# Strassen's scheme for both feed-forwards of a hybrid streaming encoder step

## The chip, the cores and the metric

One core of one Trainium2 chip runs the whole program. The metric is device time in microseconds (us) of one execution, the median of the runs. PE is the TensorE matmul engine, PEld its weight load, DVE the VectorE, ACT the ScalarE, POOL the GpSimd and SP the SyncE, whose queue issues all DMAs here.

## The reference

One encoder layer for 1024 prompt tokens and 64 sample tokens (1088 columns together), model width 1024, hidden width 2816, all in float32:

```
h = x + 1/2 * SwiGLU_1(RMSNorm(x))
h = h + concat(A, B, C) @ w_out          # gated units, pooling, gated delta rule
h = h + CrossAttn(RMSNorm(h))
h = h + 1/2 * SwiGLU_2(RMSNorm(h));  y = RMSNorm(h)
swiglu(h) = (silu(h @ w_gate) * (h @ w_up)) @ w_down
```

The two SwiGLU blocks are what changes. The norm's factor of a token is applied after the gate and up products, its gain to the operand before them.

## The kernel before, in words

Activations lie with features on partitions: a tile is 128 features by 1088 tokens. x has 8 tiles, the hidden layer 22. A float32 product is made of three products of two float32r parts, high x high, high x low and low x high (`mm3`, L219; its matmul is L224, the line of nearly all of PE's work). Tokens go in three chunks `CH` of 364, 362 and 362 columns, one PSUM bank each. A weight unit of 512 columns is loaded by SP (`load`, L195) and cut into its two parts by `weights` (L200): ACT copies the high part (`copy_act`, L159), DVE subtracts it for the low part (`tt`, L171). `product` (L210) makes 128 output columns from two units and the eight tiles of x.

`ffn` (L328) goes through the 22 hidden tiles in pairs. `gate(f)` (L332) makes a product, multiplies it by the norm's factor from PSUM (DVE, L171), applies Silu (ACT, L337) and multiplies once more (POOL, L171). `up(f, sg)` (L341) makes the other product, multiplies it in (DVE) and cuts the hidden tile (ACT, DVE). Then the pair's share of the down product is added to all eight tiles of h, which stay in SBUF (`stt`, L174, DVE from PSUM). In the last pair `done` prepares what follows: `done1` (L383) the mixers' operand, `done_att` (L1128) the second feed-forward's operand, by `split_x` (L258) and `add_square` (L264). In the second feed-forward the last pair goes chunk by chunk (`CF`), so that the final norm can begin.

Between the feed-forwards lie the mixers (L459) and the cross-attention (L1038), whose last step is `project` (L1135): `residual` adds its products to h by tiles of m, half 0 and half 1 (steps W0 and W1 of `ORDER2`).

The program's order on each engine is set by a planner that takes instructions by program order and by when it thinks them ready; each engine then runs its own list strictly in order. The first loads and cuts are written out by hand (`LOADS`, `CUTS`). Buffers are rings: an allocation waits for the last reader of the place.

Of the kernel before, what the change touches and what calls it, by code (L numbers as in the profile page):

```python
# [15 lines left out]
P = 128  # L16
TP = 1024          # prompt tokens
TS = 64            # sample tokens
# [10 lines left out]
WR = 3  # L29
WS = 4  # L30
CV = 8
NC = 2
# [26 lines left out]
RS = 3  # L59
EX = 1  # L60
XT = 2
HB = 9
LOADS = "v0 x00 g0 x01 u0 x02 x1 x2 x3 g1 u1 x4 x5 x6 x7 c0"
CUTS = "x00 g0 x01 u0 x02 x1 s0 x2 s1 x3 s2 g1 x4 u1 s3 x5 s4 x6 s5 x7 s6 s7"
A0 = (2, 4, 6, 7)
A1 = (6,7)
# [29 lines left out]
class Pool:  # L96
    """Tiles of 9 * 2^k columns: sizes that nest, so that the packing of SBUF leaves no gaps."""
# [4 lines left out]
    def tile(self, shape, dt, **kw):  # L102
        cols, c = 1, 9
        for n in shape[1:]:
            cols *= n
        while c < cols:
            c *= 2
        t = self.pool.tile([shape[0], c], dt, **kw)[:, :cols]
        return t.rearrange("p (a b) -> p a b", b=shape[2]) if len(shape) > 2 else t


class Slots:
    """Small tiles within a large one, each tag's in turn."""
# [4 lines left out]
    def tile(self, shape, dt, name, tag=None, bufs=1):  # L118
        cols = 1
        for n in shape[1:]:  # L120
            cols *= n
        ring = self.tags.setdefault(tag or name, [])
        if len(ring) < bufs:
            t = self.t[:, self.end:self.end + cols]
            self.end += cols
            ring.append(t.rearrange("p (a b) -> p a b", b=shape[2]) if len(shape) > 2 else t)
        else:
            ring.append(ring.pop(0))
        return ring[-1]


@with_exitstack
def encoder_step(ctx: ExitStack, tc: tile.TileContext, a):
# [16 lines left out]
    def banks(main, small, norm="sp"):  # L150
        """The eight PSUM banks, divided between the large products and the rest."""
# [18 lines left out]
    def tt(eng, out, in0, in1, op):  # L170
        eng.tensor_tensor(out=out, in0=in0, in1=in1, op=op)  # L171
# [22 lines left out]

    def load(src, w=512, tag="wr", bufs=WR):  # L195
        r = wp.tile([P, 528], F32, name=tag, tag=tag, bufs=bufs)
        sp.dma_start(r[:, :w], src)
        return r

    def weights(src, w=512, r=None):  # L200
        """A weight unit of w columns, loaded and cut exactly into two float32r parts."""
        if r is None:
            r = load(src, w)
        hi = wp.tile([P, 528], F32R, name="wh", tag="wh", bufs=WS)
        lo = wp.tile([P, 528], F32R, name="wl", tag="wl", bufs=WS)
# [4 lines left out]
    def product(units, x, chunks=CH):  # L210
        """w.T x for 128 columns of w and eight tiles of x, in PSUM banks by chunk."""
# [7 lines left out]
    def mm3(pp, w, c0, x, first, last, chunks=CH, m=P):  # L219
        """out += w.T x in float32: three products of the float32r parts, over all chunks."""  # L220
# [4 lines left out]

    def segs(s, n):
        """A chunk's columns as runs within the prompt or the sample: (in chunk, token, length)."""
# [4 lines left out]
    # ------------------------------------------------------------ constants  # L232
    fixed = const.tile([P, C_N + V_N + P + 1 + 264 + 8 * P], F32, name="fixed")
    cst, rest = fixed[:, :C_N], fixed[:, C_N:]
# [3 lines left out]
    row, rest = rest[:, :264], rest[:, 264:]  # L238
    wsg = rest[:, :4 * P].rearrange("p (h f) -> p h f", f=P)
    bsg = rest[:, 4 * P:6 * P].rearrange("p (t f) -> p t f", f=P)  # L240
    wpl = rest[:, 6 * P:].rearrange("p (t f) -> p t f", f=P)
# [16 lines left out]
    def split_x(src, g, slots, s=0, w=NT):  # L258
        hi, lo = (t[:, s:s + w] for t in slots)
        copy_act(hi, src[:, s:s + w], g)  # L260
# [3 lines left out]
    def add_square(acc, src, first, s=0, w=NT, eng=pool):  # L264
        """acc += src * src"""
        if first:
            act.activation(out=acc[:, s:s + w], in_=src[:, s:s + w], func=ACTF.Square)
            return
        sq = cvtile()[:, :w] if w > 512 else npool.tile([P, 512], F32, name="sq", tag="sq", bufs=3)[:, :w]
        act.activation(out=sq, in_=src[:, s:s + w], func=ACTF.Square)  # L270
        tt(eng, acc[:, s:s + w], acc[:, s:s + w], sq, ALU.add)

    def inv_rms(acc, rs=None, chunks=CH):
        """1/rms of every token, on all partitions."""
# [8 lines left out]
    def rms_tile():  # L283
        return npool.tile([P, NT], F32, name="rs", tag="rs", bufs=RS)
# [14 lines left out]
    def rows_tile():  # L299
        rt = npool.tile([P, 9], F32, name="rt", tag="rt", bufs=3)  # L300
# [3 lines left out]
    def all_rows(rt, rs):  # L304
        """A scalar of each token, tokens on partitions: on all partitions."""
        for c0, c1, w in ((0, 4, P), (4, 8, P), (8, 9, TS)):
            dg = npool.tile([P, 512], F32, name="sq", tag="sq", bufs=3)
# [20 lines left out]
    def ffn(h, x, rs, wg, wu, wd, done, chunks=None, first=None):  # L328
        with ExitStack() as fc:
            fp = mk("ffn", fc)  # L330

            def gate(f):  # L332
                sg = cvtile()[:, :NT]
                pp = first[0] if f == 0 and first else product([wg[f, 0], wg[f, 1]], x)
                for i, (s, n) in enumerate(CH):
                    tt(dve, sg[:, s:s + n], pp[i][:, :n], rs[:, s:s + n], ALU.mult)
                act.activation(out=sg, in_=sg, func=ACTF.Silu)  # L337
                tt(pool, sg, sg, rs, ALU.mult)
                return sg

            def up(f, sg):  # L341
                pp = first[1] if f == 0 and first else product([wu[f, 0], wu[f, 1]], x)
                for i, (s, n) in enumerate(CH):
                    tt(dve, sg[:, s:s + n], pp[i][:, :n], sg[:, s:s + n], ALU.mult)
                hi = fp.tile([P, NT], F32R, name="fh", tag="fh", bufs=4)
                lo = fp.tile([P, NT], F32R, name="fl", tag="fl", bufs=4)
                copy_act(hi, sg)
                tt(dve, lo, sg, hi.bitcast(F32), ALU.subtract)
                return hi, lo

            sg = gate(0)
            for f0 in range(0, NF, 2):
                # the next group's first product runs while this one's last operand is made
                hid = [up(f0, sg), up(f0 + 1, gate(f0 + 1))]
                if f0 < NF - 2:
                    sg = gate(f0 + 2)
                if f0 == NF - 2 and chunks:
                    # the last one chunk by chunk, so that what follows can begin
                    ws = [weights(wd[f0 // 2, mm]) for mm in range(4)]
                    for s, n in chunks:  # L360
                        for m in range(8):
                            pp = [main_ps()]
                            for j in range(2):
                                mm3(pp, ws[m // 2], j * 256 + (m % 2) * P, hid[j], j == 0, j == 1, ((s, n),))
                            stt(h[m][:, s:s + n], pp[0][:, :n], 0.5, h[m][:, s:s + n], ALU.mult, ALU.add)
                            done(m, s, n)
                    continue
                for mm in range(4):
                    w = weights(wd[f0 // 2, mm])
                    for m in (2 * mm, 2 * mm + 1):  # L370
                        pp = [main_ps() for _ in CH]
                        for j in range(2):
                            mm3(pp, w, j * 256 + (m % 2) * P, hid[j], j == 0, j == 1)
                        for i, (s, n) in enumerate(CH):
                            stt(h[m][:, s:s + n], pp[i][:, :n], 0.5, h[m][:, s:s + n], ALU.mult, ALU.add)
                        if f0 == NF - 2:
# [949 lines left out]
```

## Time and profile before

| | |
|---|---|
| median of 3 runs | 2359.32 us (2356.23 to 2359.63) |
| profiled execution, span | 2359.1 us (no other time of that execution is given) |
| instructions | 35138 |
| TensorE granted clock | 9 tenths or more of full speed in all 40 slices of the page |
| DMA | 144.31 MB, 61 GB/s on average |

Rows of groups read as: line, engine, operation, output <- inputs by the program's names (pp: main PSUM tiles, wr: raw weights, wh and wl: their parts, x: operand tiles, h: residual tiles, cv: work tiles), shapes, count, busy time and mean of one, then the idle time before them and what ended it. A release marked "<-DVE h L171" means that the engine sat idle until that instruction finished.

### The profile page before, as it was taken

What the parts mean: (1) busy time and instruction counts of PE and PEld (TensorE: products, weight loads), DVE (VectorE), ACT (ScalarE), POOL (GpSimd) and SP (SyncE); (2) the same over time, 40 slices, a digit from 0 to 9 for tenths busy, and PEclk for the clock granted to TensorE, in tenths of its full rate; (3) what the DMA queues carried; (4) which work ended last, traced back from release to release, by engine and by line L of the source; (5) the groups of instructions that cost most, each with busy time, mean ns of one, the idle gap of its engine ahead of it and who ended that gap; (6) DMA issues with size and microseconds to landing.
All of it is one profiled execution on the core that took longest, in us unless ns stands there. A gap on an engine that the chain in (4) does not pass through costs nothing.

```text
span 2359.1 us, 35138 instructions
## 1 busy us (share of the span) xinstructions
PE 2322.1 (98%) x14161; PEld 2258.7 (96%) x14161; DVE 1214.2 (51%) x2754; ACT 680.6 (29%) x1375; POOL 280.6 (12%) x231
## 2 busy tenths in 40 slices
PE   9999999999999999999999999999999999999997
PEld 8999999999999999898888999899999999999997
DVE  6443343443344657786867565864333334333346
ACT  5111111111111466545544444631111111111113
POOL 2000000000000210110230120110000000000005
PEclk9999999999999999999999999999999999999999
DMA  5111111111111212111114431311111111111102
GB/s 173 45 45 41 47 43 41 50 45 46 42 40 45 104 49 84 46 38 57 61 54 149 170 134 42 115 50 45 46 45 45 41 45 45 45 45 45 41 23 76
DMA packets 82166, 144.31 MB, mean 61 GB/s; under 512 B 14916, under 2 KB 28364, under 8 KB 82004
## 3 DMA queue, kind: packets, MB, share of 16 engines
q1 hardware_dynamic: 82004, 142.07, 18.7%
q8 instruction: 111, 1.82, 0.3%
q14 instruction: 51, 0.42, 0.1%
HBM read 119.19 MB, written 22.85 MB: 60 GB/s over the span
## 4 chain that ended last, share of the span: by engine, by line
PE 94%; DVE 4%; ACT 1%; DMA 1%; issue 0%; SPq 0%; POOL 0%; DVEq 0%; POOLq 0%; ACTq 0%
PE pp L224 83%; PE aux L490 1%; DVE x L174 1%; PE g L738 1%; PE g L733 1%; DVE wl L171 1%; DVE yo L174 1%; PE po L1106 1%; PE sc L1092 1%; PE pp L962 0%; PE g L715 0%; DVE pw L171 0%; PE sw L772 0%; PE sw L768 0%; PE sw L776 0%
## 5 line engine op out<-in xcount | busy, mean ns | idle before, releaser
L224 PE MATMUL pp<-x,wh 128*128 128x362 f32 (+2 forms) x6016 | 1220.3, 333 | 12.2 <-DVE h L171 5.2
L224 PEld LDWEIGHTS pp<-x,wh 128*128 128x128 f32 x6016 | 1025.1, 190 | 24.8 <-issue 5.5
L224 PE MATMUL pp<-x,wl 128*128 128x364 f32 (+2 forms) x3008 | 694.0, 333 | 0.0
L224 PEld LDWEIGHTS pp<-x,wl 128*128 128x128 f32 x3008 | 525.2, 190 | 4.3 <-issue 2.2
L159 ACT ACTIVATE wh<-wr 128x512 fp32r<-128x512 f32 (+2 forms) x360 | 207.4, 612 | 706.7 <-PE pp L224 513.8
L174 DVE SCALAR_TENSOR_TENSOR h<-pp,h 128x364 f32<-128x364 f32 (+3 forms) x528 | 250.6, 529 | 216.5 <-PE pp L224 216.5
L171 DVE TENSOR_TENSOR wl<-wr,wh 128x512 fp32r<-128x512 f32 (+2 forms) x360 | 276.7, 773 | 120.0 <-ACT wh L159 119.5
L171 POOL TENSOR_TENSOR cv<-cv,rs 128x1088 f32<-128x1088 f32 x44 | 111.4, 2533 | 1384.1 <-ACT cv L337 1244.2
L171 DVE TENSOR_TENSOR cv<-pp,rs 128x362 f32<-128x362 f32 (+2 forms) x225 | 100.9, 493 | 336.0 <-PE pp L224 336.0
L224 PE MATMUL pp<-fh,wh 128*128 128x362 f32 (+4 forms) x1056 | 240.1, 331 | 3.2 <-DVE h L174 3.1
L224 PE MATMUL pp<-fl,wh 128*128 128x362 f32 (+4 forms) x1056 | 240.3, 331 | 0.0
L224 PE MATMUL pp<-fh,wl 128*128 128x362 f32 (+4 forms) x1056 | 239.8, 331 | 0.0
L171 DVE TENSOR_TENSOR cv<-pp,cv 128x364 f32<-128x364 f32 x129 | 61.1, 529 | 270.7 <-PE pp L224 270.7
L224 PEld LDWEIGHTS pp<-fh,wh 128*128 128x128 f32 x1056 | 184.7, 189 | 4.4 <-DVE h L174 3.9
L224 PEld LDWEIGHTS pp<-fl,wh 128*128 128x128 f32 x1056 | 184.7, 189 | 0.7 <-DVE fl L171 0.2
L224 PEld LDWEIGHTS pp<-fh,wl 128*128 128x128 f32 x1056 | 184.7, 189 | 0.4 <-issue 0.2
L159 ACT ACTIVATE fh<-cv 128x1088 fp32r<-128x1088 f32 x44 | 48.9, 1112 | 381.2 <-DVE cv L171 381.2
L337 ACT ACTIVATE cv<-cv 128x1088 f32<-128x1088 f32 x44 | 49.1, 1115 | 226.3 <-DVE cv L171 226.2
L171 DVE TENSOR_TENSOR fl<-cv,fh 128x1088 fp32r<-128x1088 f32 x44 | 56.9, 1293 | 28.7 <-ACT fh L159 28.7
L171 POOL TENSOR_TENSOR acc<-acc,cv 128x1088 f32<-128x1088 f32 x16 | 43.2, 2703 | 213.3 <-ACT cv L270 206.1
L174 DVE SCALAR_TENSOR_TENSOR x<-h,fixed,x 128x1088 fp32r<-128x1088 f32 (+2 forms) x40 | 58.9, 1475 | 14.4 <-ACT x L161 14.1
L161 ACT ACTIVATE x<-h,fixed 128x1088 fp32r<-128x1088 f32 (+2 forms) x40 | 40.6, 1015 | 46.4 <-DVE h L171 28.8
(293 smaller groups left out, 1680.4 us busy)
## 6 DMA issues: line engine op xcount, KB each, us to landing
wr<-in_wd SPq DMA_DIRECT2D x88, 256.0 KB, 2.6
wr<-in_wg SPq DMA_DIRECT2D x86, 256.0 KB, 2.6
wr<-in_wu SPq DMA_DIRECT2D x86, 256.0 KB, 2.6
wr<-in_win SPq DMA_DIRECT2D x40, 256.0 KB, 2.7
h_dram<-h SPq DMA_DIRECT2D x16, 544.0 KB, 2.9
cv<-h_dram SPq DMA_DIRECT2D x16, 544.0 KB, 5.9
cv<-y_dram SPq DMA_DIRECT2D x8, 544.0 KB, 4.9
wr<-in_wout SPq DMA_DIRECT2D x16, 256.0 KB, 5.3
```

Of the source, the lines that this page charges most:

```text
L159: act.activation(out=out, in_=in_, func=ACTF.Copy)
L161: act.activation(out=out, in_=in_, func=ACTF.Copy, scale=scale)
L171: eng.tensor_tensor(out=out, in0=in0, in1=in1, op=op)
L174: dve.scalar_tensor_tensor(out=out, in0=in0, scalar=s, in1=in1, op0=op0, op1=op1)
L224: pe.matmul(pp[i][:, :n], l[:, c0:c0 + m], r[:, s:s + n], start=f, stop=e)
L337: act.activation(out=sg, in_=sg, func=ACTF.Silu)
L490: pe.matmul(pv[:n, :264], l[:, i * P:i * P + n], r[:, c:c + 264], start=f, stop=e)
L733: pe.matmul(p1[:n, loc[j]], cm[:n, loc[j]], e[:n, loc[j]], start=True, stop=True)
L738: pe.matmul(p2[:n, loc[j]], d[:n, loc[j]], t2[:n, loc[j]], start=True, stop=True)
L1092: pe.matmul(p[:, i * 256:(i + 1) * 256], l[:, sl], r[:, 0, :], start=f, stop=e)
L1106: pe.matmul(po[:, :256], l[:, 1, mt * P:(mt + 1) * P], r[:, msl], start=f and mt == 0, stop=e_ and mt == 1)
```

## The change

A pair of hidden tiles, the two halves of the tokens (544 columns each) and the two halves of the contraction form 2 x 2 blocks. Strassen's scheme in Winograd's form makes the block product of seven block products instead of eight, from sums of weight blocks (e, f, s, g: made by POOL for each unit) and of activation blocks (t1 to t4: made once by DVE, cut into two parts as all operands are).

- Gate and up: each is `blocks4` over `seven` with four tiles of x per block, in chunks `HC` of 272 columns, two PSUM banks per product, all eight banks as one ring of four products. The results are put together by DVE (from PSUM) and POOL.
- The first pair of the first feed-forward stays plain, in four quarters of 272 columns, while x still arrives; the sums of x follow it (`operand`, which loads x again).
- The hidden pair is not used at once. `hidden` cuts its seven blocks and stores them in DRAM. The down product is a phase of its own after all pairs (`GRP` = 2 pairs at a time), which loads the blocks again, 14 of 128 x 1088 per group, and h as well. The 11th pair goes without the scheme, as before.
- Before the second feed-forward, `done_att` stores h and builds the blocks as tiles m and m + 4 become ready (`PAIRED` order); the second weight block of attention's output product has two raw places for three and three part places for four.
- SBUF is laid out anew: rings at fixed places in two lasting tiles take the place of pools. Squares of DVE in `done1` go from tiles 6, 7 to tile 7. Mixers, attention and the final norm do the same operations as before.

```diff
+HC = ((0, 272), (272, 272))
+SEVEN = (("a", "11", 1), ("e", "t1", 5), ("f", "t2", 6), ("s", "22", 3), ("g", "t3", 7), ("b", "21", 2), ("d", "t4", 4))
...
+    def sums(tmp, u1, u2, v1, v2, gu=None, gv=None, new=None, done=lambda key, t: None):
...
+        t1 = tmp()
+        tt(dve, t1, u1, u2, ALU.subtract)
+        keep("t1", t1, gu)
+        t3, t2 = tmp(), tmp()
+        if gu is None:
+            tt(dve, t3, v2, u2, ALU.subtract)
+            tt(dve, t2, t3, u1, ALU.add)
...
+        keep("t2", t2, -1.0)
+        keep("t3", t3)
+        t4 = tmp()
...
+        keep("t4", t4, -1.0)
...
+                elif name == "e":
+                    raw["e"] = total(a21, a22)
+                elif name == "f":
+                    raw["f"] = total(a11, raw["e"])
+                elif name == "s":
+                    raw["s"] = total(a12, raw["f"])
+                elif name == "g":
+                    raw["g"] = total(a11, a21)
...
+                anchors["ACT"] = act.activation(out=h3, in_=raw[name], func=ACTF.Copy)
+                tt(dve, l3, raw[name], h3.bitcast(F32), ALU.subtract)
...
+    def seven(get, xb, col, after):
+        n = len(xb)
+        for wn, key, name in SEVEN:
+            pp = [main_ps() for _ in HC]
+            wh, wl = get(wn)
+            for k in range(n):
+                xh, xl = xb[k][key]
+                for l, r, f, e in ((wh, xh, True, False), (wh, xl, False, False), (wl, xh, False, True)):
+                    for p, (s, w) in zip(pp, HC):
+                        pe.matmul(p[:, :w], l[:, col(k):col(k) + P], r[:, s:s + w], start=f and k == 0, stop=e and k == n - 1)
+            after(name, [(p[:, :w], slice(s, s + w)) for p, (s, w) in zip(pp, HC)])
...
+        def after(name, pp):
+            if name in (1, 5):
+                kept[name] = room.as_()
+                for p, c in pp:
+                    copy_act(kept[name][:, c], p)
+            elif name == 6:
+                kept["u"] = add(room.as_(), pp, kept[1])
+                kept["12"] = place(0, 1, None)
+                tt(pool, kept["12"], kept["u"], kept[5], ALU.add)
+            elif name == 3:
+                put(0, 1, 1.0, add(kept["12"], pp, kept["12"]))
+            elif name == 7:
+                add(kept["u"], pp, kept["u"])
+                t = place(1, 1, kept[5])
+                tt(pool, t, kept["u"], kept[5], ALU.add)
+                put(1, 1, -1.0, t)
+            elif name == 2:
+                put(0, 0, 1.0, add(place(0, 0, kept[1]), pp, kept[1]))
+            else:
+                put(1, 0, -1.0, add(place(1, 0, kept["u"]), pp, kept["u"]))
...
+        room.second()
+        h = room.h
+        for m in PAIRED:
+            sp.dma_start(h[m], src(m))
+        for p0 in range(0, NP - 1, GRP):
+            hb = []
+            for p in range(p0, p0 + GRP):
+                for i, key in enumerate(KEYS):
+                    sp.dma_start(room.key(key, p % 4).bitcast(F32), hid_dram[p, :, i * NT:(i + 1) * NT])
+                hb.append(Blocks(room, p % 4))
+            for mm in range(2):
...
+                for par in range(2):
+                    m = 2 * mm + par
...
+                        for p, c in pp:
+                            stt(t[:, c], p, -0.5 if name == 4 else 0.5, t0[:, c], ALU.mult, ALU.add)
+                        for eng, src, b, op in more.get(name, ()):
+                            tt(eng, block(*b), block(*b), room.keep[src], op)
+
+                    more = {6: ((dve, 1, (0, 0), ALU.add), (pool, 6, (0, 1), ALU.add), (pool, 5, (0, 1), ALU.add), (dve, 5, (1, 1), ALU.subtract)),
+                            7: ((pool, 6, (1, 1), ALU.subtract), (pool, 6, (1, 0), ALU.subtract))}
+                    seven(get, hb, lambda k: k * 256 + par * P, after)
```

## Rows read from the trace of the kernel before

**Rows 1.** The page's first part: busy time, share of the span, instructions
```profile
PE 2322.1 (98%) x14161; PEld 2258.7 (96%) x14161; DVE 1214.2 (51%) x2754; ACT 680.6 (29%) x1375; POOL 280.6 (12%) x231
```

**Rows 2.** The page's chain that ended last: shares by engine, by line
```profile
PE 94%; DVE 4%; ACT 1%; DMA 1%; issue 0%; SPq 0%; POOL 0%; DVEq 0%; POOLq 0%; ACTq 0%
PE pp L224 83%; PE aux L490 1%; DVE x L174 1%; PE g L738 1%; PE g L733 1%; DVE wl L171 1%; DVE yo L174 1%; PE po L1106 1%; PE sc L1092 1%; PE pp L962 0%; PE g L715 0%; DVE pw L171 0%; PE sw L772 0%; PE sw L768 0%; PE sw L776 0%
```

**Rows 3.** Busy time by stretches of 72 us, feed-forward pairs; columns in the first line
```profile
core 0: us, PE busy (x) PEld busy (x) DVE busy (x) ACT busy (x) POOL busy (x), PEclk, DMA share, GB/s
172.00:244.00 72.00, 72.00 (x434) 72.00 (x434) 28.82 (x50) 11.03 (x16) 5.07 (x2) 1.00 0.15 44
```

**Rows 4.** The same view for line L224 alone, 600 us of feed-forward
```profile
core 0: us, PE busy (x) PEld busy (x), PEclk, DMA share, GB/s
100.00:700.00 600.00, 600.00 (x3602) 600.00 (x3602) 1.00 0.14 45
```

**Rows 5.** The same view for line L490, matmuls of 264 columns
```profile
844.30:852.30 8.00, 8.00 (x66) 8.00 (x67) 1.00 0.14 33
```

**Rows 6.** Timeline of DVE and POOL from 198 us: start, duration (us), instruction
```profile
198.18 0.68 DVE L171 TENSOR_TENSOR wl<-wr,wh 128x512 fp32r<-128x512 f32 x1
199.49 2.53 POOL L171 TENSOR_TENSOR cv<-cv,rs 128x1088 f32<-128x1088 f32 x1 [45.40 <-ACT cv L337]
199.96 2.60 DVE L171 TENSOR_TENSOR wl<-wr,wh 128x512 fp32r<-128x512 f32 x1 [1.10 <-ACT wh L159]
```

**Rows 7.** Timeline of DVE and POOL from 223 us
```profile
223.55 2.54 POOL L171 TENSOR_TENSOR cv<-cv,rs 128x1088 f32<-128x1088 f32 x1 [21.54 <-ACT cv L337]
223.84 1.42 DVE L174 SCALAR_TENSOR_TENSOR h<-pp,h 128x364 f32<-128x364 f32 x3 [0.98 <-PE pp L224]
```

**Rows 8.** Groups of instructions of the whole run, by shape
```profile
L174 DVE SCALAR_TENSOR_TENSOR h<-pp,h 128x362 f32<-128x362 f32 x336 | 162.6, 525 | 0.0
L171 POOL TENSOR_TENSOR cv<-cv,rs 128x1088 f32<-128x1088 f32 x44 | 111.4, 2533 | 1384.1 <-ACT cv L337 1244.2 <-DMA wr<-in_wu 90.9 <-DMA wr<-in_wg 43.4
L171 POOL TENSOR_TENSOR accf<-accf,sq 128x448 f32<-128x448 f32 x6 | 6.9, 1156 | 13.8 <-ACT sq L270 13.4
L159 ACT ACTIVATE wh<-wr 128x512 fp32r<-128x512 f32 x340 | 198.7, 621 | 704.4 <-PE pp L224 513.8 <-issue 176.1 <-DMA wr<-in_wmv 3.7
```

**Rows 9.** Instructions on in_wg: issue on SP, ns min/median/max, first and last start
```profile
L197 SPq DMA_DIRECT2D wr<-in_wg x86: 327/328/430, 20.3 to 2229.1; - x86
```

**Rows 10.** Busy time by stretches at the start, DMA share and GB/s last
```profile
5.00:10.00 5.00, 3.55 (x10) 2.81 (x11) 2.99 (x5) 2.29 (x4) 0.00 (x0) 1.00 0.96 322
10.00:15.00 5.00, 4.88 (x28) 4.54 (x28) 2.70 (x2) 4.77 (x5) 0.39 (x1) 1.00 1.03 417
```

**Rows 11.** The page's DMA issues: count, KB each, median us from issue to landing
```profile
h_dram<-h SPq DMA_DIRECT2D x16, 544.0 KB, 2.9
cv<-h_dram SPq DMA_DIRECT2D x16, 544.0 KB, 5.9
```

**Rows 12.** Timeline of PE at the start: the wait for x, the norm after the first products
```profile
23.84 1.07 PE L224 MATMUL pp<-x,wh 128*128 128x364 f32 x3 [2.06 <-DVE x L174]
...
36.97 2.04 PE L292 MATMUL sp<-fixed,cv 128*128 128x1 f32 x18
```

**Rows 13.** Busy time of the stretch from attention to the second feed-forward, columns as in Rows 3
```profile
1520.00:1550.00 30.00, 24.78 (x127) 23.82 (x125) 29.83 (x34) 19.31 (x25) 13.99 (x5) 0.89 0.18 54
```

**Rows 14.** Timeline of DVE in that stretch
```profile
1521.80 2.78 DVE L171 TENSOR_TENSOR wl<-wr,wh 128x256 fp32r<-128x256 f32 x1
...
1524.95 3.14 DVE L174 SCALAR_TENSOR_TENSOR x<-h,fixed,x 128x1088 fp32r<-128x1088 f32 x1
```

**Rows 15.** Timeline of PE after an idle of 3 us, end of the first feed-forward
```profile
802.53 0.66 PE L224 MATMUL pp<-fh,wl 128*128 128x364 f32 x3
...
806.79 1.11 PE L224 MATMUL pp<-fh,wh 128*128 128x362 f32 x2 [3.07 <-DVE h L174]
807.69 1.11 PE L224 MATMUL pp<-fl,wh 128*128 128x364 f32 x3
808.60 1.11 PE L224 MATMUL pp<-fh,wl 128*128 128x364 f32 x3
...
811.32 1.11 PE L224 MATMUL pp<-fh,wl 128*128 128x364 f32 x3
```

**Rows 16.** Busy time by stretches, the same microseconds, columns as in Rows 3
```profile
807.00:812.00 5.00, 5.00 (x17) 4.85 (x18) 2.93 (x6) 4.79 (x5) 2.45 (x1) 0.50 0.54 223
```

More of the change, by code (lines that the diff above doesn't have):

```diff
@@ L28 @@
 BB = 16
-WR = 3
-WS = 4
 CV = 8
@@ new lines, in blocks4, with add @@
+    def blocks4(room, get, xb, col, place, put):
+        kept = {}
+        def add(t, pp, other):
+            for p, c in pp:
+                tt(dve, t[:, c], p, other[:, c], ALU.add)
+            return t
+        def after(name, pp):
[16 more added lines that the diff above has]
+                put(0, 0, 1.0, add(place(0, 0, kept[1]), pp, kept[1]))
+            else:
+                put(1, 0, -1.0, add(place(1, 0, kept["u"]), pp, kept["u"]))
+        seven(get, xb, col, after)
@@ L237, in encoder_step @@
     eps, rest = rest[:, :1], rest[:, 1:]
[L238 to L241, printed above, removed]
+    rows_, rows_used = [rest[:, 9 * i:9 * i + 9] for i in range(4)], []
     pool.memset(ones, 1.0)
@@ L326, in parts @@
             done(m, s, n)
[L328 to L334, printed above, removed]
-                for i, (s, n) in enumerate(CH):
[L336 to L376, printed above, removed]
-                            parts(done, m)
@@ L391, in done1 @@
         if m == 7 and s + n == NT:
[L392 to L400 removed]
+            rt.append(rows_tile())
+            inv_rms_rows(acc2, rt[0], 0, NT)
+            mixer["rs"] = rms_tile()
+            all_rows(rt[0], mixer["rs"])
+    with banks(8, {}):
+        p = small_ps()
+        for _ in range(WARM):
+            pe.matmul(p[:, :P], ones, ones, start=True, stop=True)
+        first = [[main_ps() for _ in QC] for _ in range(2)]
+        ws, raw = {}, {}
+        room = Room()
+        room.weights()
+        rs = rms_tile()
+        room.sums(rs)
+        acc, sqs = room.two(2), [room.two(o) for o in (0, 4)]
+        xb = [Blocks(room, k) for k in range(4)]
+        places = [lasting[:, 2048 + NT * i:2048 + NT * (i + 1)] for i in range(3)] + [room.two(10)]
+        h = [places[i % 4] for i in range(8)]
@@ L441, in encoder_step, with operand @@
+            first[which] = out
         rt0 = rows_tile()
         inv_rms_rows(acc, rt0, 0, NT)
-        all_rows(rt0, rs)
+        all_rows(rt0, rs, [t[:, :512] for t in room.as_.places[1:]])
+        def operand():
+            h = lasting[:, 3616:3616 + NT], room.two(4)
+            for m in range(4):
+                for i in range(2):
+                    sp.dma_start(h[i], a["x"][m + 4 * i])
+                sums(room.tb, *two(h[0]), *two(h[1]), *(vec[:, V_FFN1 + i:V_FFN1 + i + 1] for i in (m, m + 4)), new=xb[m].get)
@@ new lines, in encoder_step @@
+        first.append(operand)
+        ffn(lambda m: a["x"][m], room, xb, rs, a["wg1"], a["wu1"], a["wd1"], done1, first=first)
+        x, rs, rt = x2, mixer["rs"], rt[0]
+    with ExitStack() as mc:
+        mc.enter_context(banks(MP, {k: v for k, v in dict(sw=SW, so=SO_, aux=AUX, **{f"g{i}": 1 for i in range(PG)}).items() if v}, NM))
+        dn = mk("dn", mc)
+        mp, chain = Slots(lasting[:, 3096:4224]), Slots(lasting[:, 528:1680])
+        pre = mp.tile([P, 9, 8], F32, name="pre")
+        sc = {}
+        for nm in ("beta", "gg", "gc", "egc", "nbg", "kgs", "egl"):
+            sc[nm] = mp.tile([P, 9, NH], F32, name=nm)
+        gg, gc = sc["gg"], sc["gc"]
+        sm = mp.tile([P, NH, TS], F32, name="sm")
+        junk = chain.tile([P, P], F32, name="junk")
+        mc.enter_context(behind("SP", "POOL", "ACT"))
+        unit_places((4224, 4752, 0), 0, 528, 4)
+        rnd = lasting_r[:, 4224:4480]
+        row = lasting[:, 1680:1944]
+        rest = lasting[:, 1944:3096]
+        wsg = rest[:, :4 * P].rearrange("p (h f) -> p h f", f=P)
+        bsg = rest[:, 4 * P:6 * P].rearrange("p (t f) -> p t f", f=P)
+        wpl = rest[:, 6 * P:8 * P].rearrange("p (t f) -> p t f", f=P)
```

445 lines of the change are left out of this document (351 added, 94 removed).

## The prediction

> **What bounds the kernel now.** I read the page's busy times first: TensorE (PE) 98%, VectorE (DVE) 51%, GpSimd (POOL) 12% [rows 1]. Busy PE alone proves little, so the chain that ended last comes next: 94% of the span is PE, 83% the one matmul line L224 [rows 2]. Then one period of the steady feed-forward, a pair of hidden tiles: 72.0 us hold 432 matmuls (the row's count takes in two at the edges), while DVE works 28.8 us, ScalarE (ACT) 11.0 and POOL 5.1 [rows 3]. In 600 us of it 3602 matmuls start, 166.7 ns each for 362.7 columns on average, at the full granted clock (2.4 GHz) [rows 4]. So PE is the bound by issue rate, with cover of more than half of every other engine's time. The two feed-forwards are 2 x 11 such pairs, 1584 of the 2359 us.
>
> **The change, part by part.** All sums are against the profiled execution, span 2359.1 us; it lies 0.2 us from the median, 2359.32, and no other time around it is given.
>
> *Price of a 272-column matmul.* Before shows none. The nearest row below is 264 columns: 8.00 us for 66, 121.2 ns [rows 5]. Scaled by columns this gives 124.9 ns, and 166.7 x 272/362.7 gives 125.0. I take 125, nearest to the 264 row; the ends are the rows themselves, 121 (43 us less over 10800 matmuls) and 167 (the last rival). *A page's price.* The Trainium skill, "TensorE: Matmul & The Clock Gate", Back-to-back issue gap, gives N/2.4 + 2.5 ns, 115.8 ns here and 153.6 for what runs today, where the row has 166.7. By it the saving below would be an estimated 165 us in place of 186; the rows decide.
>
> *Gate and up.* A pair costs 2 x 2 x 72 = 288 matmuls = 48.0 us now. After, gate and up are seven block products each of 4 x 3 x 2 = 24 matmuls: 336 x 0.125 = 42.0 us. This holds for 10 pairs of the first feed-forward and 11 of the second; the first pair stays plain (384 x 0.125 = 48.0, no change). Saved: 21 x 6.0 = 126 us.
>
> *Down.* A pair costs 144 matmuls = 24.0 us. After, two pairs cost four passes of seven products of 12 matmuls, 336, or 168 per weight unit row (`mm`): 21.0 us. Ten pairs in each feed-forward: 20 x 3.0 = 60 us. PE alone therefore gives 186 us.
>
> *What the other engines get.* Elementwise work grows, and two rows say how it is paid. A 512-wide DVE subtraction with both inputs in SBUF takes 0.68 us; the next one begins while a POOL product runs, takes 2.60 and ends 0.54 us after POOL [rows 6]. Three DVE operations that read PSUM run beside an equal POOL product in 1.42 us, undisturbed [rows 7]. So SBUF-to-SBUF work of DVE and POOL's work exclude one another, PSUM work of DVE does not. Prices: DVE with two SBUF inputs 0.55 us (512), 0.58 (544), at most the 0.68 of [rows 6] and 0.72 by scale; DVE from PSUM, 272 wide, 1.42/3 x 272/363 = 0.35, at most 0.525, the price of a lone 362 [rows 7, 8]; POOL between 448 columns at 1.16 and 1088 at 2.53 [rows 8]: 1.29 (512), 1.36 (544).
>
> Per pair of gate and up (42.0 us of PE): POOL makes 8 weight sums (10.3) and 8 half tiles (10.9) = 21.2. DVE cuts 14 weight blocks (7.7) and does 19 half-tile operations (4 gate, 4 up, 7 low parts, 4 sums: 11.0) = 18.7 with two SBUF inputs, and 20 from PSUM = 7.0. Run one after the other these are 46.9 us, above PE; the most that can overlap is the 7.0. With s the share of the PSUM work that falls beside POOL, a pair takes 46.9 - 7.0s, and PE is the bound only for s over 0.70. POOL is busy half the time, so chance alone gives s = 0.5; the eight PSUM banks hold four products (12 us) of slack, which smooths more. I take 43.0 us, s about 0.56.
>
> Per weight unit row of down (21.0 us of PE): POOL 4 sums + 8 half tiles = 16.1; DVE 7 cuts + 4 half tiles = 6.2 on two SBUF inputs, 20 from PSUM = 7.0. Serial 29.3, fully overlapped 22.3: here POOL is the bound even at best. POOL is the one behind, so nearly all PSUM work falls beside it: I take 22.8.
>
> ACT stays covered: about 14 x 0.62 [rows 8] and 19 smaller, some 19 of 42 us. SP issues 14 stores and 8 loads per pair; at 0.33 us each [rows 9] they fit. DMA: down reads 14 blocks of 0.557 MB and 2.1 MB of weights in 45 us, 220 GB/s; the start shows 322 and 417 [rows 10]. I cost it at nothing; were that ceiling lost, each us of load over 45 shows as PE idle.
>
> So: 21 x (43.0 - 48.0) = -105 and 20 x (22.8 - 24.0) = -24.
>
> *New edges.* (a) After the plain pair, t1 to t4 of all of x are built from reloaded tiles through one pair of buffers: four rounds of a load (5.9 us, as L987's [rows 11]) and eight DVE operations, about 43 us. The loads can begin when the first cuts are done, near 27 us of the 37 that the first products take [rows 12], so t1 of the last tile stands some 5 us after the second pair's second product wants it: +5, between 0 and 35 (if DVE's queue has them behind the plain pair). (b) Attention's last output products. Now 30 us there hold 24.8 us of PE, DVE is full [rows 13], and two of its operations sit behind POOL squares [rows 14]. After, DVE per pair of tiles: residuals 2.7, eleven half-tile cuts and sums 6.4, weights 0.8; with two squares 42 us in all, 12.7 us of POOL squares partly added, 49. PE has 27 us of work up to the product that waits for t1: 18 to 19 idle where 5 are idle now. An idle of 3 us has been followed by five triples at 0.91 us for 0.50 [rows 15], with 0.50 of the clock granted [rows 16], the 1.2 GHz level; that cost comes today too, so I add none. +14, between 5 and 30. (c) Gate/up to down, twice: the second product's weight place is free only when the last product ends, and its cut (ACT, DVE) takes 1.3 us; DVE's lag is paid here: +4 each. (d) Start, mixers and tail: same work, +2. Sum +29.
>
> Total: 2359.1 - 105 - 24 + 29 = 2259.
>
> **The rivals.** *PE stays the bound everywhere* (42.0 and 21.0): -186 + 29 = 2202. For it: [rows 3], more than half of DVE idle. Against it: the serial sums above, which need s over 0.70 in one stage and cannot hold in the other unless POOL holds its inputs for less than its rows.
>
> *Queue order.* SP is served in order. If the eight loads of h (4.5 MB, 13 us at the rates of [rows 10]) are queued ahead of the first block loads and wait for the last pair's hidden tiles (some 3 us), each change of phase costs 16 us more; and in gate/up the ring of two hidden blocks waits for stores (2.9 us to land [rows 11]), DVE standing at its head, 1 us per pair. 2 x 16 + 21 = +53: 2312. For it: DVE and SP take instructions in order; against: the planner orders by due time.
>
> *Slower: the lock pays nothing back.* Place: DVE and POOL in both stages. If DVE always stands before POOL with an SBUF operation at the head, s = 0: 46.9 and 29.3 us, 21 x -1.1 + 20 x 5.3 + 29 = +112: 2471. The sum is 112 - 287s, so the kernel is slower from s below 0.39. For it: [rows 6, 14] show the whole wait each time. Against: POOL's share alone gives s 0.5 to 0.7. The Trainium skill, "SBUF — State Buffer", Who interferes with whom, says that a DVE instruction with two SBUF inputs and a GpSimd one that reads SBUF exclude each other for a whole instruction, whoever comes first; the trace agrees (0.68 against 2.60 us).
>
> *It does not do what it says:* if a 272-wide matmul cost 143 ns, the seventh product saved would be gone, and with +29 the time 2388. The pace of today's shapes [rows 4, 5] leaves little room.
>
> **How the numbers follow.** Forecast 0.36, PE-bound 0.27, queue order 0.21, lock 0.10, no cheaper matmul 0.02; 0.04 for sums near zero, most of it "same" (within 0.2%, 4.7 us, is about what a measurement of this kernel can tell from no change). Faster 0.85, same 0.03, slower 0.12. The range takes in PE-bound with its +29 a little lower, and queue order with (a) or (b) at the upper end: 2198 to 2355. The predicted time is the forecast's, 2259.
>
> **What would show it.** In the changed profile: 272-column matmuls at 125 ns where dense; PE's periods of 42 to 44 us per pair and 21 to 23.5 per unit row; DVE subtractions with means well over 0.68 us and POOL at some 40% of the span; PE idle put down to DVE after the attention (about 20 us) and near 65 us. PE periods of exactly 42.0 and 21.0 show the first rival; idle of over 15 us before the first down product the second; periods over 46 and 25 the third. Matmuls over 130 ns (54 us) would make the whole sum wrong.

## The result, and the profile after

The changed kernel takes 2591.76 us in the median of four runs (2586.81 to 2595.72), the kernel before 2359.47 beside it: ratio 1.0984, 95% interval 1.0966 to 1.1002. It is 232 us slower where 100 us less were forecast; the time lies far above the range.

The first part of the page, and the engines' shares of the chain that ended last, of the kernel after:

```profile
PE 2304.4 (89%) x15745; PEld 2168.5 (84%) x15745; DVE 1843.9 (71%) x3534; ACT 967.1 (37%) x2083; POOL 1036.9 (40%) x768
...
PE 36%; DVE 26%; POOL 13%; DMA 11%; issue 8%; ACT 6%; SPq 0%; DVEq 0%; POOLq 0%; ACTq 0%
```

Against [rows 1, 2], PE's share of the chain falls from 94% to 36%, and DVE and POOL hold 39% of it. PE is still busy for 89% of the span, which again proves little by itself.

Busy time by stages of the kernel after (columns as in Rows 3): the plain pair, gate and up, and down with the last unit of the first feed-forward; mixers and attention; the last attention products with the next operand; gate and up, and down to the end, of the second.

```profile
5.00:68.00 63.00, 58.14 (x409) 55.65 (x410) 50.23 (x67) 38.80 (x60) 15.01 (x8) 0.92 0.55 184
68.00:588.00 520.00, 457.24 (x3374) 437.03 (x3372) 398.44 (x544) 175.95 (x342) 241.24 (x163) 0.97 0.37 129
588.00:897.00 309.00, 266.44 (x1812) 255.51 (x1812) 197.41 (x350) 84.41 (x170) 190.49 (x128) 0.91 0.51 185
897.00:1625.00 728.00, 690.41 (x4323) 625.02 (x4323) 502.20 (x1536) 355.25 (x898) 108.96 (x136) 0.96 0.25 80
1625.00:1700.00 75.00, 48.89 (x256) 46.00 (x254) 64.25 (x102) 35.76 (x55) 13.79 (x6) 0.80 0.29 102
1700.00:2255.00 555.00, 500.83 (x3702) 480.68 (x3700) 423.71 (x573) 184.59 (x362) 261.62 (x178) 0.98 0.36 123
2255.00:2593.00 338.00, 279.07 (x1862) 265.42 (x1862) 207.48 (x366) 89.91 (x196) 205.26 (x143) 0.89 0.46 169
```

The same view of the kernel before, by the same stages (each feed-forward is one):

```profile
5.00:815.00 810.00, 803.20 (x4774) 799.84 (x4775) 355.08 (x574) 158.86 (x221) 79.85 (x35) 0.99 0.17 55
815.00:1511.00 696.00, 685.32 (x4433) 630.57 (x4432) 498.67 (x1562) 354.76 (x903) 102.16 (x128) 1.00 0.26 86
1511.00:1545.00 34.00, 28.78 (x155) 27.98 (x154) 32.12 (x41) 18.75 (x23) 11.95 (x5) 0.90 0.19 55
1545.00:2359.00 814.00, 801.02 (x4790) 796.77 (x4788) 328.24 (x580) 145.78 (x224) 85.58 (x48) 0.99 0.15 45
```

So the first feed-forward takes 892 us for 810 (+82), the middle 728 for 696 (+32), the step from attention to the second feed-forward 75 for 34 (+41), the second feed-forward 893 for 814 (+79): +234, the difference of the spans. All four stages lose.

Steady stretches give the cost of a pair and of a unit row (the 168 matmuls of one weight unit in down, "row" below): gate and up from 200 to 500 us, down from 620 to 800, of the kernel after.

```profile
200.00:500.00 300.00, 269.71 (x1996) 257.90 (x1995) 230.20 (x314) 98.86 (x195) 139.79 (x96) 0.98 0.34 118
...
620.00:800.00 180.00, 155.62 (x1089) 149.60 (x1088) 111.55 (x205) 44.70 (x99) 116.55 (x77) 0.92 0.57 211
```

A pair of 336 matmuls takes 300/1996 x 336 = 50.5 us (48.0 before, 43.0 forecast), a row of 168 takes 180/1089 x 168 = 27.8 us (24.0 before, 22.8 forecast). No engine fills either stretch. In the first, DVE's and POOL's busy times add up to 370 us in 300. That is more than the stretch, in part because work overlaps and in part because a record of an engine that is held up grows longer, as [rows 6] showed. Laid over each other, the records of the two engines leave 27.4 of the 300 us with neither at work, and 10.3 of the 180 us in down.

Groups of that gate and up stretch (200 to 500 us), then its longest waits and those of the down stretch (620 to 800; columns: total us, times, longest):

```profile
L190 DVE TENSOR_TENSOR lasting<-fixed,lasting 128x512 fp32r<-128x512 f32 x83 | 80.7, 977 | 17.3 <-ACT lasting L385 17.3
L357 POOL TENSOR_TENSOR fixed<-fixed 128x512 f32<-128x512 f32 x48 | 70.3, 1464 | 25.6 <-DMA fixed<-in_wg 15.6 <-issue 8.1 <-DMA fixed<-in_wu 0.5
...
L190 DVE TENSOR_TENSOR rt<-rt,fixed 128x544 f32<-128x544 f32 x15 | 19.4, 1296 | 0.0
```
```profile
POOL rt L190 <- ACT rh L180: 72.8, 5, 15.8
...
ACT lasting L385 <- POOL fixed L357: 32.6, 12, 3.6
...
DVE rt L190 <- POOL rt L190: 16.7, 4, 4.3
```
```profile
DVE rt L193 <- POOL rt L190: 38.9, 20, 6.9
DVE fixed L193 <- POOL fixed L190: 27.6, 6, 7.7
...
POOL rt L190 <- DVE fixed L193: 20.1, 11, 3.5
```

Two things stand in these rows. First, DVE's weight cut takes 977 ns in the mean, for 0.68 us undisturbed [rows 6]. Second, the engines wait for each other's results. In gate and up POOL idles up to 15.8 us at a half tile whose place still waits for the previous pair's cuts, and the next weight sums stand behind it in POOL's order. The timeline of DVE and POOL shows the end of such a wait:

```profile
300.30 0.68 DVE L190 TENSOR_TENSOR lasting<-fixed,lasting 128x512 fp32r<-128x512 f32 x1
...
300.55 1.65 POOL L190 TENSOR_TENSOR rt<-rt 128x544 f32<-128x544 f32 x1 [15.83 <-ACT rh L180]
300.90 1.88 DVE L190 TENSOR_TENSOR rh<-rt,rh 128x544 fp32r<-128x544 f32 x1
...
302.16 5.18 POOL L357 TENSOR_TENSOR fixed<-fixed 128x512 f32<-128x512 f32 x3
```

After 15.83 us idle POOL starts, DVE's next operation takes 1.88 us, and three weight sums follow in one lump. In down, DVE's reads of PSUM wait 66.5 of 180 us for POOL's additions to the same blocks, and POOL waits 20.1 us for DVE's. POOL also waits there 22.8 us for weight loads; that the DMA is not the bound is seen below, where the kernel with all on DVE moves 224 GB/s in down for 211 here.

### The profile page after: what moved, and what is told of

Its sections match the earlier page's. It is cut to its first block, busy times and chain, and to the rows that moved or that the text cites. A ratio compares the mean times of both kernels' runs of the same rounds, so it can differ in the third digit from the quotient of the medians.

```text
span 2593.5 us, 42275 instructions
## 1 busy us (share of the span) xinstructions
PE 2304.4 (89%) x15745; PEld 2168.5 (84%) x15745; DVE 1843.9 (71%) x3534; ACT 967.1 (37%) x2083; POOL 1036.9 (40%) x768
## 4 chain that ended last, share of the span: by engine, by line
PE 36%; DVE 26%; POOL 13%; DMA 11%; issue 8%; ACT 6%; SPq 0%; DVEq 0%; POOLq 0%; ACTq 0%
PE pp L245 16%; PE pp L403 10%; POOL rt L190 10%; DVE rt L190 7%; DVE lasting L190 6%; DMA hid_dram<-rh 5%; DVE rt L193 4%; DMA fixed<-in_wd 2%; DVE rh L190 1%; DMA fixed<-in_wg 1%; POOL fixed L190 1%; DVE fixed L193 1%; DVE xb L193 1%; ACT lasting L385 1%; POOL fixed L357 1%
## 5 line engine op out<-in xcount | busy, mean ns | idle before, releaser
L403 PE MATMUL pp<-xb,lasting 128*128 128x272 f32 x9456 | 1317.9, 299 | 195.8 <-DVE lasting L190 62.6
L403 PEld LDWEIGHTS pp<-xb,lasting 128*128 128x128 f32 x9456 | 1258.3, 196 | 253.9 <-DVE lasting L190 87.8
L190 DVE TENSOR_TENSOR lasting<-fixed,lasting 128x512 fp32r<-128x512 f32 (+2 forms) x510 | 477.1, 941 | 103.5 <-ACT lasting L385 75.6
L245 PE MATMUL pp<-x,lasting 128*128 128x362 f32 (+2 forms) x2688 | 529.3, 342 | 18.1 <-DVE lasting L190 8.3
L245 PEld LDWEIGHTS pp<-x,lasting 128*128 128x128 f32 x2688 | 448.9, 193 | 33.9 <-DVE lasting L190 8.8
L190 POOL TENSOR_TENSOR rt<-rt,fixed 128x544 f32<-128x544 f32 x224 | 337.7, 1514 | 296.8 <-ACT rt L636 134.2
L385 ACT ACTIVATE lasting<-fixed 128x512 fp32r<-128x512 f32 x394 | 241.0, 627 | 409.7 <-PE pp L403 229.4
L357 POOL TENSOR_TENSOR fixed<-fixed 128x512 f32<-128x512 f32 x208 | 309.3, 1487 | 198.9 <-DMA fixed<-in_wd 68.1
L403 PE MATMUL pp<-xb,rh 128*128 128x272 f32 x960 | 132.2, 294 | 4.0 <-ACT rh L385 3.0
L403 PEld LDWEIGHTS pp<-xb,rh 128*128 128x128 f32 x960 | 127.0, 193 | 5.4 <-ACT rh L385 3.6
```

The source lines that it names most:

```text
L190: return eng.tensor_tensor(out=out, in0=in0, in1=in1, op=op)
L245: pe.matmul(pp[i][:, :n], l[:, c0:c0 + m], r[:, s:s + n], start=f, stop=e)
L357: anchors["POOL"] = pool.tensor_tensor(out=t, in0=u, in1=v, op=ALU.add)
L385: anchors["ACT"] = act.activation(out=h3, in_=raw[name], func=ACTF.Copy)
L403: pe.matmul(p[:, :w], l[:, col(k):col(k) + P], r[:, s:s + w], start=f and k == 0, stop=e and k == n - 1)
```

## The experiments

Theory, called *lock* in the expectations: POOL's slow sums exclude DVE's operations on SBUF and keep them waiting in order. Rivals: stores and small rings (*ring*); POOL's results only come late (*chain*); at the edge after attention, SP's queue order. All kernels start from the changed one. Ratios are to the kernel before, with 95% intervals.

**All of POOL's feed-forward work to DVE.** The plain pair keeps its own.

```diff
-            anchors["POOL"] = pool.tensor_tensor(out=t, in0=u, in1=v, op=ALU.add)
+            anchors["POOL"] = dve.tensor_tensor(out=t, in0=u, in1=v, op=ALU.add)
...
-                tt(pool, kept["12"], kept["u"], kept[5], ALU.add)
+                tt(dve, kept["12"], kept["u"], kept[5], ALU.add)
...
-                    more = {6: (... (pool, 6, (0, 1), ALU.add), (pool, 5, (0, 1), ALU.add), ...
+                    more = {6: (... (dve, 6, (0, 1), ALU.add), (dve, 5, (0, 1), ALU.add), ...
```

> All sums and half tiles that GpSimd makes in the two feed-forwards go to VectorE (24 and 20... per stage: 16 per pair of gate and up, 12 per unit row of down). Lock theory (GpSimd's slow products shut VectorE's SBUF work out): VectorE has about 35 us of work per pair and 20 per unit row, so pairs fall from 50 us to 43 to 44 and unit rows from 28 to 22 to 23, the whole to some 2330 us. Ring theory (in-order engines wait for hidden-block places, that is for stores): the waits now stand at VectorE's own head, the pair stays at 50 us or more, the whole at 2590 or above.

Measured: 2333.44 us, ratio 0.9885 (0.9856 to 0.9914): 258 us less than the changed kernel, and faster than the kernel before. Its first part of the page and chain; the steady stretches of gate and up and of down; and two groups of 200 to 500 us:

```profile
PE 2194.9 (94%) x15745; PEld 2106.9 (90%) x15745; DVE 1924.6 (82%) x4110; ACT 981.4 (42%) x2083; POOL 179.5 (8%) x192
...
PE 73%; DVE 17%; DMA 5%; ACT 2%; issue 2%; POOL 1%; SPq 0%; DVEq 0%; ACTq 0%
```
```profile
200.00:500.00 300.00, 300.00 (x2396) 300.00 (x2395) 271.85 (x491) 123.78 (x233) 0.00 (x0) 1.00 0.45 155
...
540.00:720.00 180.00, 171.17 (x1329) 167.69 (x1329) 171.16 (x341) 52.69 (x118) 0.00 (x0) 1.00 0.60 224
```
```profile
L190 DVE TENSOR_TENSOR lasting<-fixed,lasting 128x512 fp32r<-128x512 f32 x100 | 68.5, 685 | 5.9 <-ACT lasting L385 5.7
...
L357 DVE TENSOR_TENSOR fixed<-fixed 128x512 f32<-128x512 f32 x56 | 38.4, 685 | 0.9 <-DMA fixed<-in_wg 0.6
```

DVE has 576 more operations and the kernel is faster. PE is full in gate and up: 300/2396 = 125.2 ns per matmul, 42.1 us per pair. A row takes 22.8 us, with DVE and PE each busy for 95% of the stretch; all that PE waits for there (540 to 720 us) is DVE's weight cuts, so DVE is the bound:

```profile
PE pp L403 <- DVE lasting L190: 8.6, 11, 2.3
```

The cut is back at 685 ns, and DVE makes a weight sum in 685 ns for which POOL took 1464. This edit takes away the exclusion and the waits for POOL's results together; it does not tell them apart.

**Only gate and up, and only the weight sums.** The same edit in part. The first moves weight sums and half tiles of gate and up and leaves down on POOL (below, its line for the weight sums); the second moves the weight sums of both stages and leaves all half tiles on POOL.

```diff
-            anchors["POOL"] = pool.tensor_tensor(out=t, in0=u, in1=v, op=ALU.add)
+            anchors["POOL"] = (pool if shape else dve).tensor_tensor(out=t, in0=u, in1=v, op=ALU.add)
```

> The same for gate and up alone; down keeps GpSimd. Lock theory: pairs 43 to 44 us, unit rows 28 as in the changed kernel, the whole some 2450 us. Ring theory: no gain, 2590 or above.

> Only the weight sums (8 per pair, 4 per unit row) go to VectorE; GpSimd keeps the half tiles. Lock theory: serial sum 41 us per pair and 26.3 per unit row, so about 45 and 25 with waits, the whole some 2410 us. Ring theory: the weights no longer stand behind GpSimd's waiting half tile, so part of the gain comes too, but the half tile still waits some 14 us per pair for its place.

Measured: 2426.52 us, ratio 1.0279 (1.0250 to 1.0309), and 2436.84 us, ratio 1.0323 (1.0293 to 1.0353). Steady stretches of gate and up, the first kernel's, then the second's:

```profile
200.00:500.00 300.00, 300.00 (x2395) 300.00 (x2394) 272.07 (x491) 124.27 (x234) 0.16 (x1) 1.00 0.45 155
```
```profile
200.00:500.00 300.00, 293.82 (x2273) 286.76 (x2272) 258.19 (x408) 115.75 (x225) 82.26 (x53) 1.00 0.40 137
```

Gate and up make up 165 of the 258 us, down the other 93. The first time is 24 us below its forecast, the second 27 above. The weight sums alone bring a pair from 50.5 to 300/2273 x 336 = 44.3 us, near the 45 expected of the lock. They stood behind POOL's waits, and they were half of POOL's work; the run does not separate these two effects.

**No stores of the hidden blocks.**

```diff
-                for i in range(2):
+                for i in range(2 if p == 0 else 0):
...
-                    sp.dma_start(room.key(key, p % 4).bitcast(F32), hid_dram[p, :, i * NT:(i + 1) * NT])
+                    sp.dma_start(room.key(key, p % 4).bitcast(F32), hid_dram[0, :, i * NT:(i + 1) * NT])
```

> Leaves out the stores of the hidden blocks of all pairs but the first, and down reads the first pair's blocks each time; so no cut of a hidden block waits for a store. Ring theory: pairs fall from 50 to 44 us, the whole by about 130 us to 2460. Lock theory: within 30 us of the changed kernel's 2592.

Measured: 2542.03 us, ratio 1.0769 (1.0738 to 1.0800), 50 us less than the changed kernel. That is neither the 2460 of the ring theory nor within the 30 us that the lock theory allowed. The steady stretch of gate and up:

```profile
200.00:500.00 300.00, 276.84 (x2107) 266.77 (x2106) 231.98 (x331) 103.60 (x204) 148.38 (x104) 1.00 0.15 45
```

The ring of two hidden blocks and its stores are a part, not the main cause: the pair still takes 300/2107 x 336 = 47.8 us. The time with neither DVE nor POOL at work falls from 27.4 to 15.1 of the 300 us, that is from 4.6 to 2.4 us per pair, most of the 2.7 us that the pair gains.

**POOL work that nobody reads.** From the kernel with all on DVE; one POOL sum behind each weight cut of gate and up, into an unused place.

```diff
                 made[name] = hi, lo
+                if not shape:
+                    tt(pool, lasting_r[:, 4608:5120], hi.bitcast(F32), hi.bitcast(F32), ALU.add)
```

> The kernel with all feed-forward work on VectorE (2333 us), and beside it 14 POOL sums of 128x512 per pair of hidden tiles in gate/up, whose result nobody reads: one follows each weight cut. They stand for POOL's load without its place in any chain. If the two engines exclude each other (lock), VectorE's 29 us of two-SBUF work per pair and POOL's 14 x 1.3 = 18 us no longer fit into 42: at least 47.5, at most 56 us per pair, 21 pairs, so 2446 to 2620 us, and VectorE's 512-wide subtraction rises from 0.685 to about 1 us in the mean. If POOL cost time only because its results came late (a chain, a queue in order), nobody waits here: within 10 us of 2333.

Measured: 2452.41 us, ratio 1.0394 (1.0376 to 1.0411), 119 us more. The steady stretch of gate and up, and its groups:

```profile
200.00:500.00 300.00, 274.65 (x2072) 269.90 (x2071) 290.83 (x436) 108.10 (x208) 115.49 (x86) 0.96 0.35 122
```
```profile
L190 POOL TENSOR_TENSOR lasting<-lasting 128x512 fp32r<-128x512 f32 x86 | 116.2, 1351 | 186.7 <-ACT lasting L385 184.3
L190 DVE TENSOR_TENSOR lasting<-fixed,lasting 128x512 fp32r<-128x512 f32 x88 | 74.8, 851 | 0.6
```

In the same stretch, all that is waited for of these sums, and a sum that begins beside a PSUM operation of DVE:

```profile
ACT lasting L385 <- POOL lasting L190: 3.6, 2, 2.4
```
```profile
365.70 0.43 DVE L190 TENSOR_TENSOR rt<-pp,rt 128x272 f32<-128x272 f32 x1
365.95 1.04 POOL L190 TENSOR_TENSOR lasting<-lasting 128x512 fp32r<-128x512 f32 x1 [1.59 <-ACT lasting L385]
```

A pair takes 48.6 us instead of 42.1, DVE is busy for 97% of the stretch, and its cut grows from 685 to 851 ns (about 1000 was expected). No result of these sums is used; only the place that a sum still reads is waited for, 3.6 of the 300 us. So this is very nearly the exclusion by itself, and the pure chain theory falls. The size is at the low end of what was expected. Undisturbed, such a sum takes 1.04 us and not the 1.3 of the expectation (it adds a tile to itself; POOL's sums of two tiles take 1.26 at best), so 38.2 us of DVE and 14 x 1.04 = 14.6 us of POOL per pair, with 0.8 us of neither, take 48.6: an estimated 5.0 us overlap, of some 7 us of PSUM work. Exclusion alone costs 6.5 us per pair here. How the 50.5 - 42.1 = 8.4 us of the changed kernel split into exclusion and waits was not measured, as the load on both engines differs.

**The step from attention to the second feed-forward.** From the kernel with all on DVE: squares to DVE, the store of h issued by POOL's queue, and both.

```diff
-A4 = (5,7)
+A4 = (1, 2, 3, 4, 5, 6, 7)
...
-            now = sp.dma_start(h3_dram[m], h3[m])
+            now = pool.dma_start(h3_dram[m], h3[m])
```

> All feed-forward work on VectorE, and also all seven squares that are summed on the way from attention to the second feed-forward (two of seven were there already). If POOL's squares hold up VectorE there, that stage (75 us, of which 34 were needed before the change) gets 5 to 15 us shorter: 2318 to 2328. If the order of SP's queue holds the stage, no change: within 4 us of 2333.

> All feed-forward work on VectorE; the eight stores of h between attention and the second feed-forward are issued by POOL's queue in place of SP's, where each stood ahead of the loads of attention's output weights until its tile was ready. If SP's order holds that stage up, it gets 12 to 25 us shorter: 2308 to 2321. If VectorE's own queue there is the bound, within 5 us of 2333.

> Both edits of the stage from attention to the second feed-forward together, all feed-forward work on VectorE. If the two costs lie one behind the other, the gains add: 2295 to 2315. If one hides the other, the time is that of the better of the two alone.

Measured: 2326.69 us, ratio 0.9864 (0.9849 to 0.9879); 2333.80, 0.9892 (0.9877 to 0.9906); 2330.24, 0.9886 (0.9871 to 0.9901). The squares give 7 us, but the interval still touches that of the kernel without the edit; the store alone gives nothing, and the two do not add: all three as expected where SP's order does not hold the stage. The first of the three is the fastest here of the kernels that leave nothing out, 1.4% faster than the kernel before. Then the block sums were left out, with the store on SP's queue (and the squares on DVE) and on POOL's (squares as in the change):

```diff
-                sums(tmp, *two(h3[m - 4]), *two(h3[m]), ...)
+                for key in ("t1", "t2", "t3", "t4"):
+                    copy_act(b[key][0], two(h3[m])[1])
+                    copy_act(b[key][1], two(h3[m])[0])
```

> The kernel of the squares on VectorE (2327 us). Between attention and the second feed-forward the block sums of the activations (t1 to t4) are left out: ScalarE copies parts of h into their places, so the second feed-forward computes on other data. This takes 30 operations, 22 us, from VectorE there, and adds 16 copies of 0.65 us to ScalarE. If VectorE's own work is the bound of that stage, it gets 14 to 22 us shorter: 2305 to 2313. If the loads, TensorE or the order on SP hold it, the time stays within 5 us of 2327.

> The kernel whose stores of h between attention and the second feed-forward go by POOL's queue (2334 us), with the block sums of the activations left out there as well (ScalarE copies parts of h in their place, so the second feed-forward computes on other data). Alone, the store edit gave nothing and leaving the sums out 4 to 6 us. If VectorE's work and SP's queue hide one another in that stage, both gone give 12 to 22 us: 2312 to 2322. If neither is the bound (the chain through the last tiles and the norm), the time stays above 2326.

Measured: 2320.82 us, ratio 0.9847 (0.9830 to 0.9863), and 2317.78, 0.9834 (0.9817 to 0.9852). The first lies between its two forecasts, the second inside its first one. Leaving the sums out gives 6 us with the store on SP (2326.69 to 2320.82, the intervals still touch) and 16 with the store on POOL (2333.80 to 2317.78). The two pairs of kernels differ in the squares as well as in the store, so it is not shown that the store makes this difference. First the stretch of the kernel with squares and store moved, then the timeline of PE, ACT and SP in the kernel without sums, with the stores on SP:

```profile
1520.00:1540.00 20.00, 14.53 (x72) 13.94 (x71) 20.00 (x32) 13.27 (x20) 2.32 (x4) 0.83 0.31 119
1540.00:1560.00 20.00, 12.75 (x62) 11.95 (x62) 20.00 (x33) 12.11 (x18) 1.59 (x3) 0.76 0.23 93
```
```profile
1522.38 8.93 SPq L1538 DMA_DIRECT2D h_dram<-h  x3
...
1527.84 4.46 ACT L179 ACTIVATE xb<-h 128x544 fp32r<-128x544 f32 x8
...
1533.85 0.70 ACT L179 ACTIVATE lasting<-fixed 128x256 fp32r<-128x256 f32 x2
...
1534.30 10.87 PE L245 MATMUL pp<-x,lasting 128*128 128x364 f32 x54 [8.81 <-ACT lasting L179]
...
1535.68 0.33 SPq L221 DMA_DIRECT2D fixed<-in_wmo  x1
1537.71 0.42 ACT L179 ACTIVATE lasting<-fixed 128x256 fp32r<-128x256 f32 x1 [3.16 <-DMA fixed<-in_wmo]
```

In the first, the stores are out of SP's way and DVE is busy for 40 of 40 us. In the second, DVE has room, and PE waits 8.81 us for a weight cut that stands in ACT's order behind eight of the copies put in for the sums; the next weight load is issued after the stores, and ACT waits 3.16 us for it. So the run tells less than it was meant to: it moves work to ACT, and what DVE's block sums cost in that stage is clear of noise only in the kernel with the stores on POOL's queue, at 16 us.

**Squares at the end of the first feed-forward.**

```diff
-A1 = (7,)
+A1 = (5, 7)
```

The second run has (6, 7).

> The kernel of the squares on VectorE, and one more square at the end of the first feed-forward (tile 5) moved from POOL to VectorE, beside tile 7. That transition idles TensorE for 13 us, 8.5 of them at its end, behind the sum of the squares. If POOL's squares delay VectorE there too, 2 to 6 us less: 2321 to 2325. If the last tile's own chain holds it, within 2 us of 2327.

> As the run before, with tile 6 in place of tile 5 (the choice of the kernel before the change). Tile 6 is the last POOL square ahead of the final one, so if the chain of squares is in order on POOL, it frees most: 3 to 8 us less, 2319 to 2324. Else within 2 us of 2327.

Measured: 2333.82 us, ratio 0.9897 (0.9878 to 0.9917), and 2331.05, 0.9890 (0.9876 to 0.9905). Both miss: no gain over 2326.69. PE's wait of 8.5 us for the last square there stays unexplained beyond the chain of the last tile.

## Why the prediction was wrong

The miss is 2592 - 2259 = 333 us: 21 x (50.5 - 43.0) = 157 for the pairs, 20 x (27.8 - 22.8) = 100 for the rows, and the edges, which make up what is left of +234 after 21 x 2.5 + 20 x 3.8: +106 where +29 was forecast, 77 too few.

**Right: PE's price.** The 272-column matmul costs 125.2 ns where PE is dense, for 125 forecast; PE's pair 42.1 for 42.0. So the saving of 186 us in PE's own work holds, though the runs here with all on DVE took some 22.5 to 23 us a row, for 21.0. The formula in the Trainium skill ("TensorE: Matmul & The Clock Gate", Back-to-back issue gap) gives an estimated 115.8 ns; the page itself calls it the gap of an isolated matmul, too low at small widths where each matmul has its weight load. The measurement decides for the rows.

**Wrong: the step that failed is the form itself**, 46.9 - 7.0s for a pair and 29.3 - 7.0s for a row, used with s = 0.56 and 0.93. It has DVE or POOL at work at every moment, and only asks how much they overlap. What was missing is a term for time in which both stand still, because one waits for a result, a place or a store that is not there yet. In gate and up neither works for 27.4 of the 300 us shown, 4.6 us per pair, against 4.7 of 300 in the run with idle POOL sums, where next to nothing is waited for. DVE alone idles for 70 of the 300 us, about 12 us per pair, POOL for more than half.

**A term mis-sized.** DVE at 0.55 and 0.58 us for two SBUF inputs, which stand in no row: 22 x 0.55 + 27 x 0.58 + 7.0 = 34.8 us for all the pair's work, where the kernel with all on DVE shows 271.85/300 x 42.1 = 38.2, 10% more. In down it is 171.16/180 x 22.8 = 21.7 for 11 x 0.55 + 12 x 0.58 + 7.0 = 20.0, 8% more. I had set aside the higher 0.68 [rows 6]. POOL's prices held: the shortest sums took 1.26 (512) and 1.33 us (544).

**What each part cost**, as an estimate. The 50.5 us of a pair lie above the form's own top of 46.9, at s = 0. With DVE's measured price that top is 25.7 x 1.10 + 21.2 = 49.5. Add the 4.6 us of neither, and 50.5 leaves 3.6 us of overlap, s about 0.5: the share taken was not far off. So of the 7.5 us by which the pair missed, 4.6 are the missing term and 2.6 the price. In down the share failed too: 13.2 x 1.08 + 16.1 = 30.4 us, with 1.6 us of neither, make 27.8 only with 4.2 us of overlap, s about 0.6. The named reason, "nearly all PSUM work falls beside it", did not hold: DVE's PSUM reads waited for POOL's sums for 66.5 of 180 us, since both add to the same block of h.

**The rivals.** "The lock pays nothing back" had the right place and the right sign, and its break-even at s = 0.39 was a real warning; 0.10 was too little for it, and its 2471 too low, for the missing term and the price; s was not 0. "PE stays the bound everywhere" came true in gate and up as soon as POOL was out of the way. Of "queue order", the hidden blocks' ring and stores cost 50 us rather than 21, in this kernel where all else waits too; its 16 us at each change of phase did not come (below). The exclusion that the Trainium skill states ("SBUF — State Buffer", Who interferes with whom) agrees with the idle sums: DVE's cut rose from 685 to 851 ns beside them.

**Edges.** (a) PE waits 11.2 us in one piece up to 82 us, and 2.7 us in three more: inside the bounds of 0 to 35, above the +5 taken. The long wait did not end at t1, as summed, but at a weight cut behind POOL's weight sums, which had waited 17.6 us for an operation of DVE's:

```profile
80.03 5.11 POOL L357 TENSOR_TENSOR fixed<-fixed 128x512 f32<-128x512 f32 x3 [17.62 <-DVE rt L193]
82.42 1.28 PE L403 MATMUL pp<-xb,lasting 128*128 128x272 f32 x4 [11.24 <-ACT lasting L385]
```

(b) +41, beyond the 30 given. DVE's work was seen, but sized at 42 to 49 us; DVE is busy for 64 of the 75 us there. The stores of h, new in SP's queue ahead of attention's weight loads, were not priced; moving them gave nothing by itself. The one clear gain, 16 us, came without the block sums; the rest of the 41 stays open. (c) PE waits some 12 us in each change to down (570 to 620 and 2240 to 2285 us), for +4 taken; part of that the steady rows lose as well. (d) Start, mixers and tail, "same work, +2", was wrong: the middle takes 32 us more with the same operations. PE waits at its start, and in the last attention heads, in the kernel after:

```profile
PE pp L513 <- DVE acc L190: 8.5, 1, 8.5
```
```profile
PE sc L1496 <- ACT kv L179: 3.9, 1, 3.9
PE sc L1496 <- DVE ql L190: 3.3, 1, 3.3
```

The middle takes 727 us in the kernel with all on DVE as well, so POOL's feed-forward work is not the cause. Whether the new order of the instructions or the smaller rings are was not tried and stays open.

**The signs named.** POOL at 40%, DVE cuts well over 0.68 us, PE idle after attention and near 65 us, periods over 46 and 25 us for the lock: all seen. Not seen were the forecast's own periods, and the second rival's idle of over 15 us before the first down product: the longest pieces near the two changes are 6.4 and 3.9 us.

## What to carry to other kernels

Before work goes to an idle engine, ask whether it holds up the one beside it, and whether either must wait for the other's result; two engines that share work in order lose both ways, and 576 operations more on the faster one were cheaper here than the help. A sum over busy times needs a term for time in which every engine of the sum waits; with it a period can come out as long as the serial sum, although work overlaps. Where removing either of two costs shows little, test the pair, and change nothing else with it.

## What the hardware showed that was not expected

Results that nobody reads are not free: 294 POOL sums of 1.375 us in the mean added 119 us to the whole run. And the exclusion is no full serialization: by estimate 5.0 us per pair overlapped, of some 7 us of DVE's PSUM work.

Idle pieces of PE go with a lower clock. The granted clock was 0.92 in the down stretch of the kernel after, with PE busy for 156 of 180 us, and 1.00 in the same stage with all on DVE, where PE was busy for 171; between attention and the second feed-forward it was 0.80, where the kernel before had 0.90 in 34 us.
